# Two-block model on one core: the tensor engine's share of a depthwise convolution, as three products of exact parts instead of one in float32

## The chip, the cores and the metric

The kernel runs on one NeuronCore of one Trainium2 chip. The core has five engines, each with its own queue of instructions: TensorE (PE, with its weight loads as PEld), VectorE (DVE), ScalarE (ACT), GpSimd (POOL) and SyncE (SP), which issues the transfers of weights. The metric is the time of one execution in microseconds (us); lower is better.

## The reference, cut to what matters

The program is a chain of two transformer blocks on 256 tokens of width 1024. The first block has two layers; the second of these has a convolution module beside a cross-attention, and then a mixture of experts. The change lies in the convolution module alone: a gated projection, a causal depthwise convolution of width 31 over 768 channels, a layer norm and a swish.

```
def conformer_conv(glu_in, dw, dw_b, ln_g, ln_b):
    a, gate = jnp.split(glu_in, 2, axis=-1)
    u = a * jax.nn.sigmoid(gate)
    u = lax.conv_general_dilated(
        u, dw[:, None, :].astype(u.dtype), window_strides=(1,),
        padding=[(CONV_WIDTH - 1, 0)], dimension_numbers=('NWC', 'WIO', 'NWC'),
        feature_group_count=CONV_DIM) + dw_b.astype(u.dtype)
    return jax.nn.silu(layer_norm(u, ln_g, ln_b))
```

## The kernel before, in words

Every large product is done as three products of parts: a float32 operand is split into a high part of type fp32r (ACT copies it, which rounds) and a low part (DVE subtracts the high part from the original), and PE adds high by high, low by high and high by low (`mm3`). The weights are split on the way: SP loads a tile `wraw`, ACT writes `whi` (L107), DVE writes `wlo` (L122); slots come free as PE uses them.

The convolution stage works in six chunks of 128 channels, c = 0 to 5, with the channels on the partitions and the 256 tokens along the free side. For a chunk, `conv_in(c)` makes the gate and the value on PE (48 fp32r products, L1197 to L1199), ACT takes the sigmoid into `sg` (L1204), and DVE multiplies into `uT` (L1205, called u(c) below). The 31 taps of the depthwise convolution are then shared out: `PT = (11, 12, 12, 12, 13, 20)` taps of a chunk go to PE, as a float32 product of a diagonal matrix `dh` with a shifted window of `uT` (L1160), and the rest to DVE, one instruction a tap (L1170 to L1176). The diagonals are made by ACT from the identity and a tap's column in `dwc` (L1151), through a generator `dg` that is advanced ("pumped") at fixed places; they are made a chunk ahead. DVE adds PE's part to its own (`tap_end`, L1208).

In the loop over c, PE runs `conv_in(c + 1)` and then `pe_taps(c)`. Between these lies the cross-attention. Its keys and queries are normalised on DVE (`kn`, L533, after a power on POOL, L367), transposed on PE (L554) and copied by ACT into `mkT` and `mqT` (L555). Its four heads are advanced inside `pe_taps(2)` and later: PE makes logits (L564), DVE takes row maxima `mx` (L576), ACT takes the exponential `p` (L579). In front of `conv_in(2)` PE also runs the projection of the queries (L417 to L419 into two banks that `kn` of the keys reads first). After the six chunks DVE and ACT form sums for the layer norm, and PE adds them up (L1302 on), with a part of the output projection `og` as filler; the mixture of experts follows.

The program is recorded in the order in which it is written, and each engine works its own list in that order: nothing reorders it.

Of the kernel before, what the change touches and what calls it, by code (L numbers as in the profile page):

```python
# [10 lines left out]
F32 = mybir.dt.float32  # L11
F32R = mybir.dt.float32r
# [3 lines left out]
AF = mybir.ActivationFunctionType  # L16
OP = mybir.AluOpType
# [6 lines left out]
T = 256  # L24
# [7 lines left out]
PT = (11, 12, 12, 12, 13, 20)  # L32
# [131 lines left out]
def two_blocks(tc, A, out):  # L164
# [14 lines left out]
    def bank(i, shape=(128, 512)):  # L179
        return psp.tile(list(shape), F32, name=f"b{i}", tag=f"b{i}", bufs=1)  # L180

    V, S, G, PE = nc.vector, nc.scalar, nc.gpsimd, nc.tensor
# [92 lines left out]
    def pool(es, name, bufs, side=None):  # L275
        return es.enter_context(tc.tile_pool(name=name, bufs=bufs, side=side, reuse_waits="tile"))
# [15 lines left out]
    ident = const.tile([128, 128], F32, name="ident")  # L292
# [49 lines left out]
    dwc = const.tile([128, 6, 31], F32, name="dwc")  # L342
# [12 lines left out]
    def pc(name, j=0, n=128):  # L355
        return P[0:n, R[name] + j:R[name] + j + 1]
# [40 lines left out]
    def split(src, hi_, lo_):  # L397
        S.activation(hi_, src, AF.Copy)  # L398
        V.tensor_tensor(lo_, src, hi_.bitcast(F32), op=OP.subtract)  # L399

    def turn(*a):
        run(turns(*a))
# [18 lines left out]
    def gemm_col(o, xt, n, tbs=(0, 1), outer=False):  # L421

        th, tl = xt
        nu = 8 // (4 if n == 256 else 2)
        na = 8 // nu

        def one(u, i, tb):
            wh, wl = u
            for kk in range(na):
                k = i * na + kk  # L430
                mm3(o[tb], th[:, k, tb * 128:tb * 128 + 128], tl[:, k, tb * 128:tb * 128 + 128],
                    wh[:, kk, :], wl[:, kk, :], k == 0, k == 7)

        if outer:
            us = W.take(nu)
            for tb in tbs:
                for i, u in enumerate(us):
                    one(u, i, tb)
                    if tb == tbs[-1]:
                        W.done(1)  # L440
                    yield
        else:
            for i in range(nu):
                u = W.take(1)[0]
                for tb in tbs:
                    one(u, i, tb)
                    if tb == tbs[-1]:
                        W.done(1)
                    yield
# [199 lines left out]
    def mq_heads(i, o, mqT, ap, Tb):  # L649

        r = heads_stats(o, 4)

        def apply():
            qn = [ap.tile([128, 4, 64], F32, name="kn") for tb in range(2)]
            for tb in range(2):
                heads_apply(o[tb], r[:, 4 * tb:4 * tb + 4], 4, qn[tb])

            def fin():
                for tb in range(2):
                    heads_turn(qn[tb], 64, 4, gsc[0:64, 1 + i:2 + i], mqT, tb, bank(Tb[tb]))  # L660
            return fin
        return apply
# [22 lines left out]
    ap = pool(ph, "att", 2)  # L685
# [27 lines left out]
    o = [bank(4), bank(5)]  # L713
# [34 lines left out]
    o = [bank(2), bank(3)]  # L748
# [33 lines left out]
    o = [bank(0), bank(1)]  # L782
# [4 lines left out]
    o = [bank(2), bank(3)]  # L787
# [335 lines left out]
    ap = pool(pa, "att2", 2)  # L1123
# [17 lines left out]
    uT = cp.tile([128, 6, 30 + T], F32, name="uT")  # L1141
    G.memset(uT[:, :, 0:30], 0.0)
    vT = cp.tile([128, 6, T], F32, name="vT")
    diag = {}
    tapb = [bank(3)] * 5

    def diagonals(c):
        diag[c] = []
        for w in range(PT[c]):
            d = ap.tile([128, 128], F32, name="dh", bufs=33)  # L1150
            S.activation(d, ident, AF.Copy, scale=dwc[:, c, w:w + 1])  # L1151
            diag[c].append(d)
            yield

    def pe_taps(c):
        b = tapb[c]
        for w, d in enumerate(diag.pop(c)):
            if w % 4 == 3:
                yield
            PE.matmul(b[:, c % 2 * T:c % 2 * T + T], d, uT[:, c, w:w + T], start=w == 0, stop=w == PT[c] - 1)  # L1160
        return b

    def dve_taps(c):

        v2 = ap.tile([128, T], F32, name="v2")
        for w in range(PT[c], 31):
            wc = dwc[:, c, w:w + 1]
            d = vT[:, c] if (w - PT[c]) % 2 == 0 else v2
            if w == PT[c]:
                V.tensor_scalar(d, uT[:, c, w:w + T], wc, pc("dwb", c), op0=OP.mult, op1=OP.add)  # L1170
            elif w == PT[c] + 1:
                V.tensor_scalar(d, uT[:, c, w:w + T], wc, None, op0=OP.mult)
            else:
                V.scalar_tensor_tensor(d, uT[:, c, w:w + T], wc, d, op0=OP.mult, op1=OP.add)
            yield
        V.tensor_tensor(vT[:, c], vT[:, c], v2, op=OP.add)  # L1176
# [10 lines left out]
    def conv_in(c, tick):  # L1187

        b = bank(1 + c % 2)
        us = W.take(2)  # L1190
        for half in range(2):
            cc = slice(half * 128, half * 128 + 128)
            ob = b[:, half * T:half * T + T]
            for i, (wh, wl) in enumerate(us):
                for kk in range(4):
                    k = i * 4 + kk
                    PE.matmul(ob, wh[:, kk, cc], th[:, k], start=k == 0, stop=False)  # L1197
                    PE.matmul(ob, wh[:, kk, cc], tl[:, k], start=False, stop=False)
                    PE.matmul(ob, wl[:, kk, cc], th[:, k], start=False, stop=k == 7)  # L1199
                if half:  # L1200
                    W.done(1)
                tick()
        sg = ap.tile([128, T], F32, name="sg")
        S.activation(sg, b[:, T:2 * T], AF.Sigmoid, bias=pc("bin", 6 + c))  # L1204
        V.scalar_tensor_tensor(uT[:, c, 30:30 + T], b[:, 0:T], pc("bin", c), sg, op0=OP.add, op1=OP.mult)  # L1205

    def tap_end(c, b):
        V.tensor_tensor(vT[:, c], vT[:, c], b[:, c % 2 * T:c % 2 * T + T], op=OP.add)  # L1208

    dg = Bg(diagonals(0))  # L1210
    conv_in(0, lambda: dg.pump(3))
    later = mem_kv(1, om, mkT, mv, ap, (7, 4))
    for c in range(6):

        dt = Bg(dve_taps(c))
        dg.finish()
        if c < 5:
            dg = Bg(diagonals(c + 1))

        def tick():  # L1220
            dg.pump(3)
            dt.pump(3)
            heads.pump(1)

        if c + 1 == MQ_AT:
            o = [bank(5), bank(6)]
            for _ in gemm_col([o[0][:, 0:256], o[1][:, 0:256]], u1, 256):
                dt.pump(2)
        if c < 5:
            conv_in(c + 1, tick)  # L1230
        if c + 1 == MQ_AT:
            later()
            later = mq_heads(1, [o[tb][:, 0:256] for tb in range(2)], mqT, ap, (7, 0))
        else:
            if c < MQ_AT:
                later = later()
        if c == MQ_AT:
            later()
            mean = bank(0)
            heads = Bg(pipeline(jobs, 2))  # L1240
        if c == 5:
            tapb.append(bank(1))
        if c == 5:
            dt.pump(4)
        for i, _ in enumerate(pe_taps(c)):
            if c == 5 and i in (1, 2):
                turn(on[i - 1], 2, mix[0], mix[1], 6, i - 1, [4 + i])
            if c == 5 and i == 2:

                PE.matmul(mean[:, 0:T], ones, vT[:, 4], start=False, stop=True)  # L1250
            heads.pump(1)
            dt.pump(3)
        if c + 1 == MQ_AT:
            later = later()
        if MQ_AT <= c < 5:
            for x in ([c - 1] if c > MQ_AT else range(c)):
                PE.matmul(mean[:, 0:T], ones, vT[:, x], start=x == 0, stop=False)
        if c == 4:
            heads.finish()
            on = []  # L1260
            for tb in range(2):
                on.append(o_norm(ap, O, rinv, 0, 4, tb))
                dt.pump(3)
        dt.finish()
        if c < 5:
            tap_end(c, tapb[c])
# [32 lines left out]
    b = bank(2)  # L1299
# [8 lines left out]
    v = work.tile([128, 16], F32, name="var", bufs=4)  # L1308
# [5 lines left out]
    dg = work.tile([128, 512], F32, name="sq")[:, 0:T]  # L1314
# [8 lines left out]
    b = bank(3)  # L1323
# [121 lines left out]
    if NY:  # L1445
# [13 lines left out]
    b = bank(5)  # L1459
# [5 lines left out]
                           op0=OP.add, op1=OP.mult)  # L1465
# [190 lines left out]
    for e, fi in steps:  # L1656
# [53 lines left out]
        if prev is None:  # L1710
            def later(a=(sg, n, ht, [6, 7])):
                turn_pairs(*a)
# [79 lines left out]
    ap = pool(ph, "sec2", 2)  # L1792
# [33 lines left out]
    o = [bank(4), bank(5)]  # L1826
# [9 lines left out]
    for i in range(2):  # L1836
        V.scalar_tensor_tensor(lamr[:, 2 * i], lamr[:, 2 * i], 1.0, lamr[:, 2 * i + 1],
                               op0=OP.mult, op1=OP.mult, accum_out=nlam[:, i:i + 1])
# [14 lines left out]
    o = [bank(2), bank(3)]  # L1853
    run_with(gemm_col(o, u2, 512), {3: lambda: lq[0]([6, 7]), 5: lambda: lq[1]([6, 7])})
    lk = [plain(o[tb], tb, skT, 1.0) for tb in range(2)]
    o = [bank(0), bank(1)]
# [54 lines left out]
    for g in range(2):  # L1911
# [37 lines left out]
        for i in range(4):  # L1949
            hh = 4 * g + i  # L1950
            c = slice(hh * 64, hh * 64 + 64)
# [226 lines left out]
```

## Time and profile before

| | |
|---|---|
| median of 3 runs | 1802.96 us (1802.8 to 1804.41) |
| the profiled execution | 1803.33 us, of which the span of the trace is 1801.5 us |
| PE busy | 1766.6 us (98% of the span) |
| DVE busy | 1461.4 us (81%) |
| ACT busy | 1227.7 us (68%) |
| POOL busy | 68.4 us (4%) |
| HBM read | 504.93 MB, 281 GB/s over the span |

Busy time is the time in which at least one instruction of an engine is running. The ends of matmuls are modelled, so the pace of PE is read from the distance between starts. A time in the rows is counted from the start of the span. The convolution stage lies at about 370 to 470 us of the span.

### The profile page before, as it was taken

The numbers are of one execution on the slowest core, as the hardware profiler recorded it, in microseconds if no ns is written. First come the engines' busy times: TensorE is split into PE (matmuls) and PEld (weight loads), VectorE is DVE, ScalarE is ACT, GpSimd is POOL, SyncE is SP. The second block draws the span as 40 slices with busy tenths as digits, with TensorE's granted clock in tenths as the row PEclk, the third lists the DMA queues.
The fourth block names the chain that finished last, engine by engine and source line by source line (L and its number), as shares of the span: only waits on it lengthen the run. The fifth ranks groups of instructions, "written<-read, shape, count | busy, mean of one in ns | idle before, by whom it ended". The sixth has DMA issues, their size and how long they took to land. (4 is left out here: it accounts for less than half of the span.)

```text
span 1801.5 us, 23486 instructions
## 1 busy us (share of the span) xinstructions
PE 1766.6 (98%) x8620; PEld 1473.5 (82%) x8620; DVE 1461.4 (81%) x1759; ACT 1227.7 (68%) x1599; POOL 68.4 (4%) x100
## 2 busy tenths in 40 slices
PE   8999999999999999999999999999999999999998
PEld 6788888889788888888888888888888878778886
DVE  6556988688699999999999999999999974477553
ACT  5645544475488878877878788778787876656442
POOL 4200000000100000000000000000000010010000
PEclk9999999999999999999999999999999999999999
DMA  8325998562599999999999999999999744237540
GB/s 294 131 83 178 398 357 305 195 209 87 193 356 387 396 358 366 388 358 379 370 370 384 365 363 383 363 370 367 370 366 367 294 146 162 76 129 266 185 157 24
DMA packets 162891, 508.64 MB, mean 282 GB/s; under 512 B 8666, under 2 KB 26162, under 8 KB 148432
## 3 DMA queue, kind: packets, MB, share of 16 engines
q1 hardware_dynamic: 159376, 497.64, 74.6%
q0 software_dynamic: 3104, 8.91, 1.5%
q8 instruction: 69, 1.13, 0.2%
q10 hardware_dynamic: 288, 0.52, 0.1%
q14 instruction: 54, 0.44, 0.1%
HBM read 504.93 MB, written 2.11 MB: 281 GB/s over the span
## 5 line engine op out<-in xcount | busy, mean ns | idle before, releaser
L122 DVE TENSOR_TENSOR wlo<-wraw,whi 128x1024 fp32r<-128x1024 f32 (+1 forms) x894 | 1055.4, 1218 | 148.9 <-ACT whi L107 116.6
L107 ACT ACTIVATE whi<-wraw 128x1024 fp32r<-128x1024 f32 (+1 forms) x894 | 932.1, 1059 | 273.4 <-PE b L418 248.2
L417 PE MATMUL b<-whi,xeh 128*128 128x512 f32 x904 | 354.7, 392 | 0.0
L419 PE MATMUL b<-wlo,xeh 128*128 128x512 f32 x904 | 352.3, 390 | 0.0
L418 PE MATMUL b<-whi,xel 128*128 128x512 f32 x904 | 352.3, 390 | 0.0
L417 PE MATMUL b<-whi,xth 128*128 128x512 f32 (+2 forms) x656 | 255.4, 389 | 6.1 <-ACT xth L398 2.1
L417 PE MATMUL b<-whi,hth 128*128 128x512 f32 x656 | 258.0, 393 | 0.4 <-ACT hth L398 0.3
L418 PE MATMUL b<-whi,htl 128*128 128x512 f32 x656 | 255.7, 390 | 0.2 <-DVE htl L399 0.2
L419 PE MATMUL b<-wlo,hth 128*128 128x512 f32 x656 | 255.6, 390 | 0.0
L419 PE MATMUL b<-wlo,xth 128*128 128x512 f32 (+2 forms) x656 | 249.3, 380 | 2.5 <-DVE wlo L122 2.5
L418 PE MATMUL b<-whi,xtl 128*128 128x512 f32 (+2 forms) x656 | 249.2, 380 | 0.9 <-DVE xtl L399 0.7
L419 PEld LDWEIGHTS b<-wlo,xeh 128*128 128x128 f32 x904 | 169.7, 188 | 35.4
L418 PEld LDWEIGHTS b<-whi,xel 128*128 128x128 f32 x904 | 169.9, 188 | 34.3
L417 PEld LDWEIGHTS b<-whi,xeh 128*128 128x128 f32 x904 | 169.9, 188 | 34.3
L417 PEld LDWEIGHTS b<-whi,xth 128*128 128x128 f32 x656 | 124.1, 189 | 30.8 <-ACT xth L398 3.2
L419 PEld LDWEIGHTS b<-wlo,xth 128*128 128x128 f32 x656 | 123.9, 189 | 27.0 <-DVE wlo L122 4.2
L417 PEld LDWEIGHTS b<-whi,hth 128*128 128x128 f32 x656 | 123.3, 188 | 25.7 <-ACT whi L107 0.5
L419 PEld LDWEIGHTS b<-wlo,hth 128*128 128x128 f32 x656 | 123.2, 188 | 25.7
L418 PEld LDWEIGHTS b<-whi,xtl 128*128 128x128 f32 x656 | 124.1, 189 | 24.3 <-DVE xtl L399 3.0
L418 PEld LDWEIGHTS b<-whi,htl 128*128 128x128 f32 x656 | 123.3, 188 | 25.0 <-DVE htl L399 0.5
L398 ACT ACTIVATE hth<-b 128x512 fp32r<-128x512 f32 (+1 forms) x83 | 45.0, 591 | 61.9 <-PE b L410 61.9
L399 DVE TENSOR_TENSOR htl<-b,hth 128x512 fp32r<-128x512 f32 (+1 forms) x83 | 53.1, 678 | 31.7 <-ACT hth L398 31.1
(389 smaller groups left out, 1419.0 us busy)
## 6 DMA issues: line engine op xcount, KB each, us to landing
wraw<-in_moe_w_gate_dram SPq DMA_DIRECT2D x112, 1024.0 KB, 7.5
wraw<-in_moe_w_up_dram SPq DMA_DIRECT2D x112, 1024.0 KB, 7.5
wraw<-in_moe_w_down_dram SPq DMA_DIRECT2D x112, 1024.0 KB, 7.5
wraw<-in_w_ff_dram SPq DMA_DIRECT2D x32, 1024.0 KB, 5.2
adw<-in_ada_w_dram SPq DMA_DIRECT2D x24, 1024.0 KB, 7.7
wraw<-in_w_in_dram SPq DMA_DIRECT2D x12, 1024.0 KB, 5.0
wraw<-in_ffn_w_gate_dram SPq DMA_DIRECT2D x11, 1024.0 KB, 6.3
wraw<-in_ffn_w_up_dram SPq DMA_DIRECT2D x11, 1024.0 KB, 8.1
```

Of the source, the lines that this page charges most:

```text
L107: nc.scalar.activation(h, r, AF.Copy)
L122: self.nc.vector.tensor_tensor(l, r, h.bitcast(F32), op=OP.subtract)
L398: S.activation(hi_, src, AF.Copy)
L399: V.tensor_tensor(lo_, src, hi_.bitcast(F32), op=OP.subtract)
L417: PE.matmul(o, xh, wh, start=first, stop=False)
L418: PE.matmul(o, xl, wh, start=False, stop=False)
L419: PE.matmul(o, xh, wl, start=False, stop=last)
```

## The change

The tensor engine's taps are computed from parts, as the projections are. `uT` of a chunk is split into a tile `uhl` of two fp32r parts (ACT copies, DVE subtracts) right behind u(c); the tap columns are split once into `dws`; a diagonal has a high part (ACT) and a low part, which ACT makes for odd taps and GpSimd for even ones. A tap is then three fp32r products instead of one float32 product. The diagonals have 13 buffers of two parts instead of 33 of one, and a chunk's diagonals are pumped in the loop body of the same chunk (while `conv_in(c + 1)` is recorded) instead of one chunk ahead. The numbers of taps, DVE's taps and all else are as before.

```
+    dws = ap.tile([128, 2, 6, 31], F32R, name="dws", bufs=1)
+    split(dwc, dws[:, 0], dws[:, 1])
+    parts = {}
+
     def diagonals(c):
         diag[c] = []
         for w in range(PT[c]):
-            d = ap.tile([128, 128], F32, name="dh", bufs=33)
-            S.activation(d, ident, AF.Copy, scale=dwc[:, c, w:w + 1])
+            d = ap.tile([128, 2, 128], F32R, name="dh", bufs=13)
+            wh, wl = (dws[:, i, c, w:w + 1].bitcast(F32) for i in range(2))
+            S.activation(d[:, 0], ident, AF.Copy, scale=wh)
+            if w % 2:
+                S.activation(d[:, 1], ident, AF.Copy, scale=wl)
+            else:
+                G.tensor_scalar(d[:, 1], ident, wl, None, op0=OP.mult)
             diag[c].append(d)
             yield
 
     def pe_taps(c):
         b = tapb[c]
-        for w, d in enumerate(diag.pop(c)):
+        o = b[:, c % 2 * T:c % 2 * T + T]
+        x = parts.pop(c)
+        for w in range(PT[c]):
             if w % 4 == 3:
                 yield
-            PE.matmul(b[:, c % 2 * T:c % 2 * T + T], d, uT[:, c, w:w + T], start=w == 0, stop=w == PT[c] - 1)
+            while len(diag[c]) <= w:
+                dg.pump()
+            d = diag[c][w]
+            mm = ((d[:, 0], x[:, 0, w:w + T]), (d[:, 0], x[:, 1, w:w + T]), (d[:, 1], x[:, 0, w:w + T]))
+            for i, (a, v) in enumerate(mm):
+                PE.matmul(o, a, v, start=w + i == 0, stop=w == PT[c] - 1 and i == 2)
         return b
...
         V.scalar_tensor_tensor(uT[:, c, 30:30 + T], b[:, 0:T], pc("bin", c), sg, op0=OP.add, op1=OP.mult)
+        x = parts[c] = ap.tile([128, 2, 288], F32R, name="uhl")
+        G.memset(x[:, :, 0:30].bitcast(F32), 0.0)
+        split(uT[:, c, 30:30 + T], x[:, 0, 30:30 + T], x[:, 1, 30:30 + T])
...
         dt = Bg(dve_taps(c))
-        dg.finish()
-        if c < 5:
-            dg = Bg(diagonals(c + 1))
+        if c > 0:
+            dg = Bg(diagonals(c))
+            dg.pump(1 if c < 5 else 13)
```

On ACT, at the end of `conv_in(2)` (its sigmoid is `sg`), the list before has the copies into `mkT` and the squares `sq` of the queries right behind `sg`:

```order
L1151 ACTIVATE dh<-ident,dwc 128x128 x3
L1204 ACTIVATE sg<-b_3617,P 128x256 [waits PE_49,Activation_49]
L555 ACTIVATE mkT<-b_3715,P 64x4x128 [waits PE_49]
L555 ACTIVATE mkT<-b_3721,P 64x4x128 [waits PE_49]
L527 ACTIVATE sq<-b_3548 128x256 [waits Activation_49]
```

and now:

```order
L1159 ACTIVATE dh<-ident,dws 128x128
L1221 ACTIVATE sg<-b_3640,P 128x256 [waits PE_49,Activation_49]
L398 ACTIVATE uhl<-uT 128x256 [waits DVE_49,Pool_49]
L555 ACTIVATE mkT<-b_3751,P 64x4x128 [waits PE_49]
L555 ACTIVATE mkT<-b_3757,P 64x4x128 [waits PE_49]
L527 ACTIVATE sq<-b_3571 128x256 [waits Activation_49]
```

Between `sg` and `mkT` there now stands the copy of the high part, with a wait on DVE. A chunk later the same copy stands in front of `mqT`, the queries for the first head. Before:

```order
L1204 ACTIVATE sg<-b_3755,P 128x256 [waits PE_49,Activation_49]
L555 ACTIVATE mqT<-b_3854,gsc 64x4x128 [waits PE_49]
L555 ACTIVATE mqT<-b_3860,gsc 64x4x128 [waits PE_49]
L579 ACT_TABLE_LOAD
L579 ACTIVATE p,rinv<-b_3870,mx 128x256 [waits DVE_49]
```

Now:

```order
L1221 ACTIVATE sg<-b_3818,P 128x256 [waits PE_49]
L398 ACTIVATE uhl<-uT 128x256 [waits DVE_49]
L555 ACTIVATE mqT<-b_3930,gsc 64x4x128 [waits PE_49]
L555 ACTIVATE mqT<-b_3936,gsc 64x4x128 [waits PE_49]
L579 ACT_TABLE_LOAD
```

On DVE, at u(2), the list now has the subtraction for the low part (L399) between u(2) (L1222, formerly L1205) and the sums of squares `ssh` that lead to `kn`:

```order
L1193 TENSOR_TENSOR vT<-vT,v_3585 128x256 [waits DVE_49]
L1222 SCALAR_TENSOR_TENSOR uT<-b_3640,P,sg 128x256 [waits Activation_49]
L399 TENSOR_TENSOR uhl<-uT,uhl 128x256 [waits Activation_49]
L528 TENSOR_REDUCE ssh<-sq 128x4 [waits Activation_49] x2
L365 TENSOR_SCALAR var<-ssh 128x8 [waits DVE_49]
L533 TENSOR_TENSOR kn<-b_3571,rst 128x256 [waits PE_49,Pool_49]
```

It waits for ACT's copy, which itself waits for u(2); everything below it on DVE stands behind this. On PE, the first head's logits (L564) stand behind three taps of chunk 2, as before:

```order
L1177 MATMUL b_3317<-uhl,dh 128x256 [waits Activation_49] x2
L1177 MATMUL b_3317<-uhl,dh 128x256
L1177 MATMUL b_3317<-uhl,dh 128x256 [waits Pool_49]
L564 MATMUL b_3952<-mkT,mqT 128x256 [waits Activation_49]
L568 MATMUL b_3952<-mkT,mqT 128x256 [waits Activation_49]
L1177 MATMUL b_3317<-uhl,dh 128x256 x5
```

PE's place for them has not moved; what they wait for has, from behind `sg` to behind the copy.

## Rows read from the trace of the kernel before

**Rows 1.** Busy time by stretch: window, length, each engine (count), PEclk, DMA share, GB/s.
```profile
core 0: us, PE busy (x) PEld busy (x) DVE busy (x) ACT busy (x) POOL busy (x), PEclk, DMA share, GB/s
380.00:460.00 80.00, 79.16 (x515) 73.67 (x514) 70.51 (x160) 47.44 (x117) 3.17 (x2) 1.00 0.32 110
600.00:1200.00 600.00, 600.00 (x2745) 498.50 (x2745) 563.23 (x539) 483.82 (x510) 4.68 (x5) 1.00 0.98 371
492.50:500.00 7.50, 5.19 (x29) 4.89 (x29) 5.96 (x19) 4.59 (x5) 0.95 (x2) 0.54 0.90 286
```

**Rows 2.** Timeline of PE in the convolution stage: start, length, line, tiles, shapes, count.
```profile
375.72 0.28 PE L1199 MATMUL b<-xth,wlo 128*128 128x256 f32 x1
375.84 0.28 PE L1197 MATMUL b<-xth,whi 128*128 128x256 f32 x1
...
387.71 0.36 PE L417 MATMUL b<-whi,xth 128*128 128x256 f32 x1 [0.84 <-DVE kn L533]
...
411.97 1.46 PE L1160 MATMUL b<-uT,dh 128*128 128x256 f32 x6
413.27 0.60 PE L564 MATMUL b<-mkT,mqT 66*128 66x256 f32 x2
...
462.24 0.50 PE L1302 MATMUL b<-ones,vT 128*128 128x1 f32 x4
```

**Rows 3.** Instructions of the taps' line L1160: duration ns min/median/max, first and last start.
```profile
L1160 PE MATMUL b<-uT,dh x160: 376/378/435, 382.0 to 459.2; 128*128 128x256 f32 x160
```

**Rows 4.** Timeline of DVE, the instructions around u(c), with idle time before them.
```profile
378.36 0.48 DVE L1205 SCALAR_TENSOR_TENSOR uT<-b,P,sg 128x256 f32<-128x256 f32 x1 [3.09 <-ACT sg L1204]
...
403.95 0.48 DVE L1205 SCALAR_TENSOR_TENSOR uT<-b,P,sg 128x256 f32<-128x256 f32 x1
...
407.05 0.76 DVE L533 TENSOR_TENSOR kn<-b,rst 128x256 f32<-128x256 f32 x2 [1.76 <-POOL rst L367]
...
414.87 0.47 DVE L1205 SCALAR_TENSOR_TENSOR uT<-b,P,sg 128x256 f32<-128x256 f32 x1
415.26 0.41 DVE L576 TENSOR_REDUCE mx<-b 128x1 f32<-128x256 f32 x1
...
444.61 0.48 DVE L1205 SCALAR_TENSOR_TENSOR uT<-b,P,sg 128x256 f32<-128x256 f32 x1 [0.45 <-ACT sg L1204]
...
449.72 0.42 DVE L1208 TENSOR_TENSOR vT<-vT,b 128x256 f32<-128x256 f32 x1 [0.63 <-PE b L1160]
...
453.81 0.42 DVE L399 TENSOR_TENSOR xtl<-b,xth 128x256 fp32r<-128x256 f32 x1 [1.10 <-ACT xth L398]
...
460.53 0.41 DVE L1208 TENSOR_TENSOR vT<-vT,b 128x256 f32<-128x256 f32 x1
```

**Rows 5.** Timeline of ACT in the stage.
```profile
370.06 1.86 ACT L1151 ACTIVATE dh<-ident,dwc 128x128 f32<-128x128 f32 x6
...
390.74 1.06 ACT L107 ACTIVATE whi<-wraw 128x1024 fp32r<-128x1024 f32 x1 [4.65 <-PE b L418]
391.71 1.85 ACT L1151 ACTIVATE dh<-ident,dwc 128x128 f32<-128x128 f32 x6
...
400.19 1.24 ACT L555 ACTIVATE mkT<-b,P 64x512 f32<-64x512 f32 x2
401.33 0.63 ACT L527 ACTIVATE sq<-b 128x256 f32<-128x256 f32 x2
...
411.99 1.24 ACT L555 ACTIVATE mqT<-b,gsc 64x512 f32<-64x512 f32 x2
...
468.48 0.42 ACT L398 ACTIVATE xth<-vT 128x256 fp32r<-128x256 f32 x1
```

**Rows 6.** Timeline of POOL in the first 70 us.
```profile
38.95 0.20 POOL L760 COPY qa<-cs 128x8 f32<-128x8 f32 x1
...
51.22 2.92 POOL L367 TENSOR_TENSOR rst<-var,mhalf 128x16 f32<-128x16 f32 x1 [11.77 <-DVE var L365]
...
66.48 3.85 POOL L367 TENSOR_TENSOR rst<-var,mhalf 128x16 f32<-128x16 f32 x1 [10.46 <-DVE var L365]
```

**Rows 7.** Timeline of DVE at 66 us.
```profile
66.35 1.22 DVE L122 TENSOR_TENSOR wlo<-wraw,whi 128x1024 fp32r<-128x1024 f32 x1
```

## The prediction

> **What bounds the kernel now.** I read the busy time by stretch first. In the convolution stage (380 to 460 us) PE is busy 79.2 of 80 us at a granted clock of 1.00, DVE 70.5 and ACT 47.4; in the mixture of experts PE is busy all 600 of 600 us, so the transfers, with a share of 0.98 there, do not hold it [rows 1]. So a microsecond taken from PE's list in this stage moves everything behind it, as long as PE then finds its inputs ready, and DVE has only 9.5 us in 80 to be late in. Then I read PE's timeline for its pace, by starts, since ends are modelled: six float32 passes from 411.97 to 413.27, 0.216 us each, and an fp32r product of the same shape every 0.12 us [rows 2]. Then the instructions on DVE and ACT around u(c), for who waits for whom there [rows 4, 5]. The reader should see that DVE runs close behind PE: u(0) waits for the sigmoid 3.09 us, `tap_end` of chunk 4 waits for PE 0.63, and DVE's last addition ends at 460.94, only 1.3 us before PE starts the sums at 462.24 [rows 2, 4].
>
> **The change, part by part.** *PE.* The 80 taps are 160 passes now [rows 3], 160 x 0.216 = 34.6 us. They become 240 products of the form that runs at 0.12 (same shapes, the same pattern of a weight loaded twice and another once), 28.8 us. PE's own list gets 5.8 us shorter.
>
> *ACT.* New are 39 low diagonals, six copies of 128x256 and one of `dws`. A diagonal costs 0.30 (six in 1.86), a copy 0.42 [rows 5]: 39 x 0.30 + 7 x 0.42 = 14.6 us on an engine that has 32 us idle in 80 [rows 1]. The amount is hidden; what isn't hidden is the order. An engine's list is worked in order: ACT stood 4.65 us before a `whi` that waited for PE, and the diagonals behind it, which need nothing from PE, began only at 391.71 [rows 5].
>
> *DVE.* Six subtractions, each behind a copy on ACT that needs u(c) complete. Before, the row behind u(3) starts 0.39 us after it although u(3) lasts 0.47 [rows 4]: rows overlap by 0.08. Now u must end, ACT copies 0.42 [rows 5] with about 0.04 for each handover (an estimate), and the subtraction occupies about 0.35 (0.42 less the overlap). Each u(c) costs DVE 0.08 + 0.42 + 0.08 + 0.35 = 0.9 us, and DVE has nothing else to do in between.
>
> I follow the delay of DVE's list against before, since it grows faster than PE's saving:
> - In front of `sg`(0) ACT does the `dws` copy and five odd low diagonals, 6 x 0.30 = 1.8; DVE waits there for `sg` today [rows 4, 5], so all of it arrives: +1.8.
> - u(0) and u(1): +0.9 each, +3.6. Behind u(1) stands `kn` of the keys, for which PE's query projection waits 0.84 us even today, until 387.71 [rows 2]. PE would be there at 386.87 less 11 taps x 0.072 = 386.1, and starts at 391.3: 5.2 us idle.
> - u(2): +0.9; and the `mkT` pair (1.24) and the `sq` pair (0.63) [rows 5], done long before DVE came to them, now stand behind ACT's copy. From the copy's end they take some 1.8; DVE fills 0.7 of that with the subtraction and the first `ssh`, and waits 1.1. Delay at `kn` of the queries (407.05, still with its 1.76 us wait for POOL): +5.6.
> - u(3), 414.87 before, comes at 420.5. Behind it `mx` used to start 0.39 later. Now the chain is u 0.48, handover and copy 0.46, `mqT` pair 1.2, PE's logits 0.86 (two of 0.43, as from 413.27 [rows 2]) and a handover, 3.1 us: +2.7, +8.3 in all. PE, 3.6 late at the projection and 0.9 faster in `pe_taps(1)`, has finished its three taps at 415.7 and stands until 422.7: 6.9 us idle.
> - u(4), u(5): +0.9 each, +10.1.
> - With PE now ahead, DVE's waits for PE's results vanish: 0.45 + 0.63 + 1.10 [rows 4] = 2.2. +7.9.
> - The sums had 1.3 us of room behind DVE: 7.9 - 1.3 = +6.6 at 462.24, and what follows is the same chain.
>
> PE's 5.8 us are thus spent in waiting. The far end on the other side: if none of DVE's delays reached the sums, -5.8.
>
> *POOL.* 41 low diagonals and six small memsets. Nothing in the trace multiplies 128x128 there; the nearest plain operation, a copy of 128x8, takes 0.20, the farthest, a power of 128x16, 2.92 [rows 6]. I take 0.2 to 0.4 for a multiplication, which is the plain kind; six or seven in a chunk's 12 us or more are then hidden. At 2.92 they would need 18 to 20 us a chunk and hold PE by some 5 each, 1830; I keep that as the far end, hardly likely.
>
> *POOL beside DVE.* The power at 66.48 began while DVE subtracted two SBUF tiles (66.35, 1.22 us), and took 3.85 instead of 2.92, 0.93 more, about what DVE's instruction still had to run [rows 6, 7]. So the two do get in each other's way; whether DVE also waits for POOL no row shows. Some 35 of the 41 multiplications fall among DVE's taps, which read two SBUF tiles each. From nothing to a whole copy each, 35 x 0.2 = 7 us; I take 1, since only the other direction is seen. The Trainium skill speaks against this change here: its page "SBUF — State Buffer", section "SBUF: two separate sides", says that a DVE instruction with two SBUF inputs contends with a GpSimd instruction that reads SBUF, and that whichever starts second is blocked for the whole of the first. By that rule DVE would lose all 35 pieces. The trace agrees as far as POOL's 0.93 us of waiting go.
>
> *Clock.* In the stage the granted clock is 1.00; in the 7.5 us from 492.5, in which PE is busy 5.19, it is 0.54 [rows 1], so about 7 us of them at 1.2 GHz. Idle times of 5.2 and 6.9 us may bring such a fall. It costs between nothing, as PE is not last in most of the stage, and 3.5 us a fall; I take 1.
>
> Sum: +6.6 + 1 + 1 = +8.6 on the profiled execution's 1803.3 us (span 1801.5 and 1.8 around it). The median shown is 0.4 lower, so 1811.5.
>
> **The rivals.** *The saving goes through (faster).* DVE's 9.5 idle us take up its 6 x 0.9 = 5.4, and the copies into `mkT` and `mqT` do not come late because u(2) and u(3) do not. The time would be 1803 - 5.8 = 1797. For it: PE is the fullest engine, ACT and POOL have room. Against it: 1.76 of DVE's idle time is POOL's power and stays. It decides at u(3): if u(3) ends before PE has done its three taps of chunk 2, the heads wait for nothing.
>
> *No change.* The start and the copies cost what I count, but the two chains behind the copy (+1.1, +2.7) are hidden, because ACT finds u(2) and u(3) done: 6.6 - 3.8 = 2.8, without blocking or clock, 1806. Against it: DVE would have to reach u(3) some 2.7 us earlier than its list allows.
>
> *POOL blocks DVE fully.* Each multiplication among the taps costs DVE 0.2: +6.6 + 7 + 1, 1818. For it speaks the power that waited at 66.48 [rows 6, 7]; against it, that no row shows DVE waiting for POOL. It decides when most multiplications find DVE in the middle of its taps. (This is how the page "SBUF — State Buffer" of the Trainium skill would have it.)
>
> *The parts don't run at 0.12.* If a product with a window that starts at any column cost 0.216, PE would need 240 x 0.216 = 51.8, +17, 1820. Against it: shapes, types and loads are those of `conv_in`.
>
> **How the numbers follow.** 1807 to 1816 as summed: 0.50, with 1811.5 as its middle. POOL blocking, slow parts or slow multiplications, 1816 and more: 0.20. About as before, 1799.4 to 1806.6: 0.16. Faster, near 1797: 0.14. A measurement of this kernel can tell 0.2% (3.6 us) from no change. So faster 0.14, same 0.16, slower 0.70. The range leaves out the faster case and the far end: 1801 to 1821; the likeliest case's own is 1807 to 1816.
>
> **What would show it.** Right: fp32r taps 0.12 apart; ACT's copies `uhl` waiting for DVE's `uT`; PE idle some 5 us before the query projection, released by `kn`, and some 7 us before the first L564, released by ACT's `mqT`; the sums (L1302 before) near 469; a fall of the clock behind one of these. Wrong: PE without such waits and the sums near 456; or DVE's taps longer or further apart than now where POOL works, which would be the blocking; or PE waiting tap by tap for POOL's low parts.

## The result and the profile after

The median of the changed kernel is 1814.99 us (1811.64 to 1815.84, 4 runs), that of the kernel before, measured beside it, 1803.12 us (1802.80 to 1804.41, 4 runs): a ratio of 1.0059, with a 95% interval of 1.0048 to 1.0071. The change made the kernel slower. The profiled execution took 1811.64 us (span 1809.9), which is 8.3 us more than the profiled execution of before, where the sum had 8.6.

The profile of the changed kernel, busy time by stretch as in [rows 1]:

```profile
core 0: us, PE busy (x) PEld busy (x) DVE busy (x) ACT busy (x) POOL busy (x), PEclk, DMA share, GB/s
380.00:460.00 80.00, 70.06 (x531) 68.78 (x531) 65.81 (x145) 52.69 (x140) 31.37 (x39) 0.91 0.27 92
390.00:397.00 7.00, 6.43 (x33) 6.46 (x34) 6.86 (x17) 1.36 (x2) 0.00 (x0) 0.56 0.24 97
420.00:427.00 7.00, 5.03 (x20) 4.66 (x21) 4.24 (x12) 3.86 (x8) 1.66 (x2) 0.51 0.47 152
500.00:508.00 8.00, 5.46 (x31) 5.07 (x31) 6.60 (x21) 4.48 (x6) 1.77 (x3) 0.62 0.79 256
```

In the 80 us in which PE was busy 79.16 us before, it is busy 70.06 now, and DVE too has fallen, from 70.51 to 65.81. No engine became the bound: PE and DVE both wait more (the work in the window is not quite the same, as the stage has shifted). The granted clock, 1.00 throughout these 80 us before, is near its lower level (1.2 GHz) from 390 to 397 and from 420 to 427; the fall that stood at 492.5 before now stands at 500.

The timeline of PE in the changed kernel, with its idle time and what ended it:

```profile
368.68 0.39 PE L1214 MATMUL b<-xth,whi 128*128 128x256 f32 x1 [0.25 <-ACT xth L398]
...
380.89 4.10 PE L1177 MATMUL b<-uhl,dh 128*128 128x256 f32 x33
390.57 0.55 PE L417 MATMUL b<-whi,xth 128*128 128x256 f32 x1 [5.58 <-ACT whi L107]
...
416.30 1.31 PE L1177 MATMUL b<-uhl,dh 128*128 128x256 f32 x9
421.97 1.22 PE L564 MATMUL b<-mkT,mqT 66*128 66x256 f32 x2 [4.36 <-ACT mqT L555]
...
423.48 4.71 PE L1177 MATMUL b<-uhl,dh 128*128 128x256 f32 x24
428.03 0.60 PE L564 MATMUL b<-mkT,mqT 66*128 66x256 f32 x2
...
471.02 0.61 PE L1322 MATMUL b<-ones,vT 128*128 128x1 f32 x4 [1.15 <-DVE vT L1228]
```

The parts run as fast as hoped: 33 products in 4.10 us, 0.12 each. Then PE stands 5.58 us before the query projection and 4.36 before the first logits (L564). The low clock falls on what comes next: the 48 products of the projection take 8.27 us to the next `conv_in` instead of 5.83, and the 24 products from 423.48 to the next logits take 4.55 us instead of some 2.9 (24 x 0.12). The sums start at 471.02, 8.78 later than before [rows 2], although this stage's first product (368.68) came 1.06 us earlier than before's (369.74).

The timeline of DVE around u(c) (L1222):

```profile
379.12 0.48 DVE L1222 SCALAR_TENSOR_TENSOR uT<-b,P,sg 128x256 f32<-128x256 f32 x1 [3.37 <-ACT sg L1221]
...
388.38 0.47 DVE L1222 SCALAR_TENSOR_TENSOR uT<-b,P,sg 128x256 f32<-128x256 f32 x1
389.33 0.42 DVE L399 TENSOR_TENSOR uhl<-uT,uhl 128x256 fp32r<-128x256 f32 x1 [0.48 <-ACT uhl L398]
389.68 0.75 DVE L533 TENSOR_TENSOR kn<-b,rst 128x256 f32<-128x256 f32 x2
...
407.84 0.42 DVE L399 TENSOR_TENSOR uhl<-uT,uhl 128x256 fp32r<-128x256 f32 x1 [0.55 <-ACT uhl L398]
409.25 0.74 DVE L528 TENSOR_REDUCE ssh<-sq 128x4 f32<-128x256 f32 x2 [0.99 <-ACT sq L527]
...
412.00 0.76 DVE L533 TENSOR_TENSOR kn<-b,rst 128x256 f32<-128x256 f32 x2 [1.79 <-POOL rst L367]
...
420.42 0.47 DVE L1222 SCALAR_TENSOR_TENSOR uT<-b,P,sg 128x256 f32<-128x256 f32 x1
421.38 0.43 DVE L399 TENSOR_TENSOR uhl<-uT,uhl 128x256 fp32r<-128x256 f32 x1 [0.48 <-ACT uhl L398]
424.08 0.42 DVE L576 TENSOR_REDUCE mx<-b 128x1 f32<-128x256 f32 x1 [2.28 <-PE b L568]
...
429.10 0.42 DVE L576 TENSOR_REDUCE mx<-b 128x1 f32<-128x256 f32 x1 [1.74 <-PE b L568]
```

And that of ACT, the copies `uhl` and what stands behind them:

```profile
388.89 0.42 ACT L398 ACTIVATE uhl<-uT 128x256 fp32r<-128x256 f32 x1 [5.48 <-DVE uT L1222]
389.21 0.39 ACT L1157 ACTIVATE dh<-ident,dws 128x128 fp32r<-128x128 f32 x1
389.50 1.04 ACT L107 ACTIVATE whi<-wraw 128x1024 fp32r<-128x1024 f32 x1
...
420.93 0.42 ACT L398 ACTIVATE uhl<-uT 128x256 fp32r<-128x256 f32 x1 [3.92 <-DVE uT L1222]
421.25 1.24 ACT L555 ACTIVATE mqT<-b,gsc 64x512 f32<-64x512 f32 x2
```

ACT stands 5.48 and 3.92 us in front of a copy that waits for DVE, with work behind it. At the second place that work is `mqT`, and this is PE's wait of 4.36 us, seen from the engine that causes it. At the first place it is a `whi`, a weight that PE needs next, and the view names it as what PE waited for. But `kn` on DVE ended only 0.1 us before it (390.43 and 390.54), and the projection started 0.14 us after the end of `kn`, just as in the kernel before (387.57 and 387.71), where no `whi` was late:

```profile
386.83 0.74 DVE L533 TENSOR_TENSOR kn<-b,rst 128x256 f32<-128x256 f32 x2
```

So the late `whi` cost PE 0.1 us at most. The first wait is DVE's lateness at `kn`; the second is ACT's queue behind the copy.

### The profile page after: what moved, and what is told of

Its sections match the earlier page's. It is cut to its first block, busy times and chain, and to the rows that moved or that the text cites. A ratio compares the mean times of both kernels' runs of the same rounds, so it can differ in the third digit from the quotient of the medians.

```text
span 1809.9 us, 23801 instructions
## 1 busy us (share of the span) xinstructions
PE 1763.2 (97%) x8700; PEld 1473.4 (81%) x8700; DVE 1465.7 (81%) x1766; ACT 1241.6 (69%) x1645; POOL 104.9 (6%) x147
## 3 DMA queue, kind: packets, MB, share of 16 engines
q8 instruction: 70, 1.15, 0.2%
## 5 line engine op out<-in xcount | busy, mean ns | idle before, releaser
L399 DVE TENSOR_TENSOR htl<-b,hth 128x512 fp32r<-128x512 f32 (+1 forms) x83 | 53.2, 678 | 31.7 <-ACT hth L398 31.1
```

## The experiments

The times of a stage can be compared between executions only from a common point. In the table the columns are the start, in us of the span, of the stage's first product, of u(0) on DVE, of the query projection, of the first logits and of the sums on PE; then the time from first product to sums; then the ratio of the time to that of the kernel before, with its 95% interval. Each row is one profiled execution, the ratio is from all its runs.

| kernel | first | u(0) | projection | logits | sums | first to sums | ratio |
|---|---|---|---|---|---|---|---|
| before | 369.74 | 378.36 | 387.71 | 413.27 | 462.24 | 92.50 | 1 |
| after | 368.68 | 379.12 | 390.57 | 421.97 | 471.02 | 102.34 | 1.0059 (1.0048 to 1.0071) |
| split_only | 369.87 | 378.49 | 389.68 | 420.36 | 472.28 | 102.41 | 1.0052 (1.0036 to 1.0067) |
| no_split | 370.43 | 380.87 | 390.50 | 417.48 | 462.98 | 92.55 | 0.9998 (0.9989 to 1.0007) |
| late_split | 368.90 | 379.34 | 390.49 | 416.98 | 464.74 | 95.84 | 1.0028 (1.0018 to 1.0037) |
| late_fix | 370.45 | 380.89 | 390.70 | 416.46 | 462.87 | 92.42 | 1.0001 (0.9992 to 1.0010) |
| low_act | 370.29 | 382.78 | 393.96 | 424.78 | 476.11 | 105.82 | 1.0074 (1.0058 to 1.0089) |
| pool_twice | 370.36 | 380.80 | 392.25 | 423.73 | 474.93 | 104.57 | 1.0057 (1.0040 to 1.0073) |
| early | 372.78 | 383.30 | 394.76 | 426.17 | 474.96 | 102.18 | 1.0075 (1.0061 to 1.0089) |
| early_late | 376.19 | 385.89 | 395.71 | 421.24 | 467.87 | 91.68 | 1.0024 (1.0015 to 1.0033) |
| before_early | 370.21 | 378.24 | 387.61 | 413.15 | 462.12 | 91.91 | 0.9998 (0.9989 to 1.0007) |
| before_spread | 371.16 | 379.47 | 389.55 | 415.14 | 464.11 | 92.95 | 1.0005 (0.9996 to 1.0014) |
| spread | 369.05 | 377.61 | 387.43 | 413.00 | 459.66 | 90.61 | 0.9993 (0.9984 to 1.0001) |
| spread_pt | 369.19 | 377.76 | 387.57 | 412.41 | 459.17 | 89.98 | 0.9990 (0.9982 to 0.9999) |

The change adds 9.84 us between the first product and the sums. The theory says that this is DVE's waiting for ACT's copy, with what the copy holds up on ACT; the main rival, that the products, the diagonals or POOL beside DVE cost it.

**split_only: the split without the products.** The taps stay float32 as before, on POOL nothing is added.

```
 V.scalar_tensor_tensor(uT[:, c, 30:30 + T], b[:, 0:T], pc("bin", c), sg, op0=OP.add, op1=OP.mult)
+x = ap.tile([128, 2, 288], F32R, name="uhl", bufs=1)
+split(uT[:, c, 30:30 + T], x[:, 0, 30:30 + T], x[:, 1, 30:30 + T])
```

> The kernel before, with its float32 taps and diagonals, and the split of u(c) added at the place where the change has it; nothing reads the parts. Theory: the waits of DVE for the copy and those behind the copy on ACT come as with the change, and PE's 5.8 us did not matter there: sums at 468 to 471, 1808 to 1813. Rival A (POOL, diagonals or products cost it): within 2 us of before, 1801 to 1805.

Measured: 1813.76 us beside 1803.81. The waits in this kernel, summed from 366 to 480 us (who waits for whom, total, times, longest):

```profile
ACT uhl L398 <- DVE uT L1205: 13.0, 6, 5.0
...
PE b L564 <- ACT mqT L555: 5.0, 1, 5.0
...
DVE uhl L399 <- ACT uhl L398: 2.9, 6, 0.5
...
PE b L417 <- DVE kn L533: 2.7, 1, 2.7
```

ACT stands 13 us in front of its six copies, and PE has the two waits again, 2.7 us before the projection and 5.0 before the logits. It cost a little more than expected (sums at 472.28). Between first product and sums the split alone adds 9.91 us and the whole change 9.84, but that the two agree so well is chance, since they are made up differently. Here u(0) is not late (8.62 us after the first product, as before), there is no low clock behind the projection (its 48 products take 5.82 us), and PE, with its longer list, comes to the sums 1.3 us after DVE's last addition: 1.83 us of wait more at the projection, 4.97 at the logits, and 2.96 at the low clock behind them (7.28 us from the first head's logits to the second's, 4.32 before) make 9.8. In the changed kernel PE waits for DVE at the sums (1.15).

**no_split: the products without the split.** The opposite half: u(c) is rounded to fp32r by DVE as it is written, and the product with the low part reads zeros, so the low part of u is left out.

```
-split(uT[:, c, 30:30 + T], x[:, 0, 30:30 + T], x[:, 1, 30:30 + T])
+V.scalar_tensor_tensor(x[:, 30:30 + T], b[:, 0:T], pc("bin", c), sg, op0=OP.add, op1=OP.mult)
...
-(d[:, 0], x[:, 1, w:w + T])
+(d[:, 0], zero[:, w:w + T])
```

> The changed kernel without the split of u(c): DVE writes u(c) rounded to fp32r at once, the taps of both engines read that, and the product with the low part of u reads a tile of zeros, so that PE has the same 240 products. The low part of u is left out of the result. Theory: without the copy and the subtraction DVE is later than before by the start (0.8 us) and POOL (1.0 us) and earlier by up to 2.2 us of waits for PE; the sums start at 461 to 462 and the time is 1800 to 1803, some 2 us less than with the late split. Rival A (POOL beside DVE, diagonals or products cost it): 1808 or more. Rival B (PE's list is the bound once DVE is relieved): 1796 to 1798.

Measured: 1803.96 us, no difference from before, a microsecond above what was expected. All 240 products, all diagonals and POOL's multiplications are in it, so rival A falls. But PE's 5.8 us do not show either. PE waits 3.78 us before the projection (0.84 before), since u(0) still comes 1.82 us later after the first product than before (10.44 against 8.62) and PE is there sooner; and behind that wait the projection's 48 products take 8.33 us instead of 5.83, at a granted clock of 0.59 over 7 us. The two together, 2.94 and 2.50 us, are nearly all of the 5.8.

**late_split and late_fix: the split elsewhere.** Same work; only the place of the split in the lists changes.

```
-split(uT[:, c, 30:30 + T], x[:, 0, 30:30 + T], x[:, 1, 30:30 + T])
+pend.append(c)
...
 def tick():
+    if pend:
+        dt.pump(3)
+        late_split()
     dg.pump(3)
     dt.pump(3)
```

> The changed kernel, but the split of u(c) into its two parts is recorded later: on DVE behind three more taps of its own, on ACT behind the copies into mkT, sq and mqT. Work on every engine is the same. Theory (the cost is the waiting for ACT's copy, and what stands behind that copy on ACT): DVE's six waits of 0.5 us for uhl go (3.0 us), and PE's waits of 5.6 us for whi before the query projection and of 4.4 us for mqT before the first logits shrink below 2 us each; no fall of the clock is left between 380 and 430 us. DVE keeps six subtractions of 0.35 (2.1), the later start (0.8) and 1.0 us of POOL beside it, less the 2.2 us that it waited for PE before: the sums start near 463 and the time is 1802 to 1805. Rival A (the cost is POOL beside DVE, or the products themselves): 1810 to 1815 as with the change. Rival B (with the waits gone PE's 5.8 us go through): 1797 to 1799.

Measured: 1807.79 us, above the expected 1802 to 1805. The wait for `mqT` is gone, but PE still waits 4.37 us for `kn`. The edit itself had moved three more of DVE's taps ahead of each u(c + 1): from u(0) to u(1) it took 9.97 us, 9.26 with the change. In late_fix those three taps take the place of the tick's own (`else: dt.pump(3)`), and chunk 5's split stands behind the first three taps in `pe_taps(4)`.

> The late split again, without moving taps: the split takes its place behind the three taps that DVE does anyway at the first tick of the next projection (the run before had moved three more taps of each chunk ahead of u of the next one), and the split of chunk 5 stands behind three taps of chunk 4 and not behind 20 diagonals on ACT. Theory: the 1.2 us of those three taps at u(1) and PE's wait of 1.6 us for the parts of chunk 5 go; the later start (1.8 us at u(0)) stays, and with it a wait of PE of 3 to 4 us before the query projection: 1804 to 1807. Rival (the rest of the loss is POOL beside DVE and the products): 1807 to 1809.

Measured: 1803.73 us beside 1803.44, just under the expected range. The timeline of PE in late_fix:

```profile
390.70 0.58 PE L417 MATMUL b<-whi,xth 128*128 128x256 f32 x1 [3.02 <-DVE kn L533]
...
416.46 0.60 PE L564 MATMUL b<-mkT,mqT 66*128 66x256 f32 x2
416.89 0.61 PE L568 MATMUL b<-mkT,mqT 66*128 66x256 f32 x2
417.15 3.21 PE L1177 MATMUL b<-uhl,dh 128*128 128x256 f32 x24
420.20 0.60 PE L564 MATMUL b<-mkT,mqT 66*128 66x256 f32 x2
```

No wait stands in front of the logits now, and with no fall of the clock there the 24 products take 3.05 us. Putting the split elsewhere took back the whole of the loss. Beside no_split, which has neither copies nor subtractions (92.55 us from first product to sums, 92.42 here), the six copies and six subtractions as such cost nothing that can be measured. Both sides of the split were moved at once, on ACT and on DVE; what each gave by itself was not run.

**low_act: all low diagonals on ACT.** POOL's multiplication becomes `S.activation(d[:, 1], ident, AF.Copy, scale=wl)`.

> The changed kernel with all 80 low diagonals on ACT and none on POOL. Theory: the 1.0 us by which DVE's taps are lengthened beside POOL goes, ACT gets 41 x 0.30 = 12.3 us more, of which some 1.8 in front of the first sigmoid: 1810 to 1815, as with the change. Rival A (POOL holds DVE up): 1806 or less, with DVE's taps at 0.39 us apart throughout.

Measured: 1817.78 us, above the expected range. DVE's taps are 0.39 to 0.40 us apart throughout, so what POOL took from them is back; but ACT has six more diagonals ahead of the first sigmoid, u(0) comes 12.49 us after the first product (10.44 with the change), and that is more than was gained. Against the change the loss is not clear of noise (the two intervals overlap).

**pool_twice: POOL's multiplications doubled.**

```
 G.tensor_scalar(d[:, 1], ident, wl, None, op0=OP.mult)
+G.tensor_scalar(twice, ident, wl, None, op0=OP.mult)
```

> The changed kernel with every low diagonal on POOL made a second time, into a tile that nothing reads: 41 more multiplications of 0.75 to 1.0 us on POOL. Theory (POOL only lengthens a DVE tap now and then: 16 of 94 taps by 0.11 us in the changed kernel, about 1.2 us of pace in all): taps that are lengthened rise to about twice, 1 to 2 us more, and PE may wait up to 1 us for a low part: 1815 to 1819. Rival (a DVE instruction is held for the whole of POOL's multiplication): more than 10 us more, 1825 or above.

Measured: 1813.79 us, a little under the expected range and within the scatter of the change itself. From first product to sums it is 2.2 us more than with the change; PE waits for a low part three times in it, 1.4 us together. The longest of DVE's taps took 0.66 us and the mean rose from 0.488 to 0.496, so the rival falls.

**early, early_late, before_early: the start, first try.** The theory of the start said that ACT had too much ahead of the first sigmoid. So chunk 0's diagonals (and `dws`) were recorded in the product before the stage, in the change (early), in late_fix (early_late) and in the kernel before (before_early).

```
+    dg = Bg(diagonals(0))
+    for i, _ in enumerate(gemm_col(om, m1_["t"], 512)):
+        if i == 2:
+            turn(xs[0], 8, u1[0], u1[1], 0, 0, [2, 3])
+        dg.pump(2)
+    dg.finish()
```

> The changed kernel with only the early diagonals of chunk 0 and the early split of the tap columns; the split of u(c) stands where the change has it. Theory: the start's 1.8 us and up to 2 us more go, the waits behind the copy on ACT (1.0 at ssh, 2.7 at the first logits) and the subtractions stay: 3 to 5 us less than the change, 1809 to 1812. Rival (the start is hidden behind PE): 1813 to 1816.

> As late_fix, and the split of the tap columns and the diagonals of chunk 0 are recorded in the product before the stage (the cross-attention's keys and values of the memory), where ACT is idle 40 per cent of the time, so that ACT has nothing but weights ahead of the first sigmoid. Theory (DVE's start sets the stage, since DVE runs close behind PE to its end): u(0) comes 1.8 us earlier than with the change and up to 2 us earlier than before, PE's wait before the query projection falls under 2 us, there is no fall of the clock behind it, and part of PE's 5.8 us goes through: 1797 to 1802. Rival (ACT's new work before the stage delays the weights that PE waits for there): 1804 or more.

> The kernel before with the same one thing: the diagonals of chunk 0 are recorded in the product before the stage. Theory: DVE starts up to 2 us earlier, but PE is busy 79.2 of 80 us there, so only PE's 0.84 us before the query projection can go: 1801.5 to 1803.5. Rival (DVE is the bound in the stage even before): 1800 to 1801.

Measured: 1817.66, 1808.87 and 1803.23 us. early lies above its range and above its rival's; early_late missed, and its rival held; before_early came out as expected. The first product of early_late:

```profile
376.19 0.58 PE L1220 MATMUL b<-xth,whi 128*128 128x256 f32 x1 [4.31 <-ACT xth L398]
```

ACT was idle there only on average: the diagonals came between the norm and the copies `xth` on which the stage's first product waits. And u(0) still came 9.70 us after it (early_late), since a weight conversion ahead of the sigmoid waited 4.49 us. From first product to sums early_late was as quick as late_fix: 91.68 us (92.42).

**spread, spread_pt, before_spread: the start, second try.** Four of chunk 0's diagonals are recorded ahead of the first sigmoid instead of all eleven: `conv_in(0, lambda: dg.pump(1))` in place of `dg.pump(3)`, in late_fix (spread) and in the kernel before (before_spread). spread_pt also moves five taps from DVE to PE: `PT = (13, 13, 13, 13, 13, 20)`.

> The late split of the run before, and of chunk 0's diagonals only four are recorded ahead of the first sigmoid on ACT, the other seven behind it. Theory: the 1.8 us by which u(0) comes later than before go, and some more (11 ACTIVATEs fewer ahead of the sigmoid than in the change); PE's wait before the query projection falls from 3.0 us to under 1.5, no fall of the clock is left behind it; DVE is then ahead by about 2 us and the sums come 2 us earlier: 1800.5 to 1802.5. Rival (a weight conversion that waits on ACT ahead of the sigmoid sets the start): u(0) no earlier than before, 1802.5 to 1804.

> As spread, and five more taps go from DVE to PE: (13, 13, 13, 13, 13, 20) instead of (11, 12, 12, 12, 13, 20). Theory: a tap costs PE 0.36 us now and DVE 0.40; with DVE late and PE waiting, five taps take 2.0 us from DVE and give PE 1.8 of the time that it stood idle: 1 to 2 us less than spread, 1799 to 1801.5. Rival (PE is the bound once the waits are gone): as spread or up to 1.8 us more.

> The kernel before with the same one thing at its start: four of chunk 0's diagonals ahead of the first sigmoid, seven behind it. Theory: PE has only 0.84 us of idle time to give back there, since it is busy 79.2 of 80 us: 1802 to 1803.5. Rival (DVE bounds the stage before, too): 1800 to 1801.5.

Measured: 1802.40, 1801.34 and 1804.36 us, the last a microsecond above what was expected. PE in spread_pt:

```profile
385.65 1.91 PE L1177 MATMUL b<-uhl,dh 128*128 128x256 f32 x13 [0.66 <-POOL dh L1161]
...
387.57 0.38 PE L417 MATMUL b<-whi,xth 128*128 128x256 f32 x1
```

The projection waits for nothing any more and runs at the full clock; PE waits 0.66 us for POOL's low part and 0.29 us for DVE at the sums. From first product to sums it takes 89.98 us, 2.52 less than before. With 85 taps its list saves 34.6 - 255 x 0.12 = 4.0 us, so more than half of that goes through. In the time that is a ratio of 0.9990 with an interval that ends at 0.9999: faster by about a thousandth, at the edge of what can be told, and not told apart from spread. The same edit of the start does nothing for the kernel before; whether the five moved taps would do something for it was not run.

## Why the prediction was right, step by step

The forecast of slower, by DVE's and ACT's waits, held, and so did the place of each. The steps against the common point (to each delay the 1.06 us are added by which this stage began earlier):

- *PE's own list, 34.6 to 28.8 us:* right in pace, 33 products in 4.10 us. The rival of slow parts is out.
- *The start, +1.8 at u(0):* 10.44 - 8.62 = 1.82.
- *+3.6 at `kn` of the keys, PE idle 5.2:* the projection came 3.92 later and PE was idle 5.58. The view names a `whi` as the releaser, which stood behind ACT's copy of u(1) and which the prediction did not follow; it came 0.1 us after `kn`, so the path that was forecast is the one that set the time.
- *+5.6 at `kn` of the queries:* 412.00 - 407.05 + 1.06 = 6.0, with DVE's wait for `sq` 0.99 (1.1 forecast).
- *+2.7 behind u(3):* mis-sized. From u(3) to `mx` it took 424.08 - 420.42 = 3.66 instead of 0.39, so +3.27: the logits ran at the low clock, 1.22 us for a pair that took 0.60 before. PE's idle time there was 4.36 instead of 6.9, because PE had lost 2.4 us at the low clock from the projection on (8.27 us to the next `conv_in`, 5.83 before).
- *The clock, +1:* too small. Behind the two waits lie two falls, and the second kept DVE waiting for the logits of the second head too (1.74 us). With the 0.6 in the step above that is some 2 us; no kernel here has waits as long as these without a fall, so the two are not fully told apart.
- *u(4), u(5), the waits that vanish and the room, +10.1, -2.2, -1.3:* held. DVE's last addition came 470.55 - 460.53 + 1.06 = 11.1 later, where the steps with POOL's and the clock's 1 us had 9.9; the surplus is mostly the clock's, above. The three waits for PE are gone, and the sums came 9.84 later, so 1.2 of the 1.3 us of room was used.
- *POOL, 0.2 to 0.4 a multiplication:* wrong by more than twice; 41 of them took 0.89 on average. It was hidden, as the step said, because POOL had the time.
- *POOL beside DVE, +1:* about right. DVE's 94 taps of this form (L1191) average 0.475 us before and 0.488 after, 1.2 us in all. The rows of the taps' line in the changed kernel (durations in ns: least, median, most):

```profile
L1191 DVE SCALAR_TENSOR_TENSOR vT<-uT,dwc,vT x49: 471/478/588, 381.9 to 466.1; 128x256 f32<-128x256 f32 x49
L1191 DVE SCALAR_TENSOR_TENSOR v<-uT,dwc,v x45: 472/479/592, 382.3 to 465.4; 128x256 f32<-128x256 f32 x45
```

  No tap is held for a whole multiplication, of which the shortest took 0.60 us; the longest tap took 0.11 us more than the median. The Trainium skill's page "SBUF — State Buffer", section "SBUF: two separate sides", would have the second of the two blocked for the whole of the first. For POOL the trace agrees in kind (up to 2.58 us instead of 0.6), for DVE's taps it does not.

Together: 9.84 us from first product to sums, where the steps gave 6.6 + 1 + 1 = 8.6. From PE's side it is the same: PE waited 10.25 us more (5.58, 4.36 and 1.15 instead of 0.84), lost 2.44 us to the low clock behind the first wait and 2.32 behind the second (6.06 us from the first head's logits to the second's, 3.74 in late_fix), and saved 5.8, which makes 9.2 of the 9.84. That the profiled execution came out at +8.3, so near to the 8.6, is partly luck: the stage began 1.06 us earlier than before's.

What stays open is the rest of the median, which came 3.5 us above the forecast 1811.5: the other three executions of the changed kernel took 1814.9 to 1815.8 us, some 3.5 more than the profiled one. Their mean granted clock was 0.991, that of the profiled one 0.993; if the missing 0.002 of 1810 us is time at the lower level, it is worth some 3.6 us (an estimate, and a rough one, as both clocks are rounded). The profile of pool_twice, at 1814.3 us of span, has two stretches at a lower clock (0.72 from 115 to 121 us and from 1586 to 1592) where the changed kernel's has 1.00, both outside this stage; that the other three had these too was not seen. The first of the two lies ahead of all that the change touches.

## What to carry to other kernels

A cheaper product on the fullest engine can gain nothing, or lose, if its operand needs a copy that stands in two in-order lists: ask, for that copy, who waits for it, what is queued behind it on its engine, and whether it could be recorded later, when its input is long there and its reader still far off. Here that alone was worth the whole loss, with not an instruction less. Then look at the start of the stage: DVE ran close behind PE, and with 1.8 us of small work moved from ahead of the first sigmoid the stage took 90.61 us instead of 92.42 (spread and late_fix, one profile each). And an engine that is idle 40 per cent of the time can still be the wrong place for new work, when its next instruction is the one that others wait for.

## What the runs showed of the hardware

- A wait of PE can cost twice. In the changed kernel, with idle times of 5.58 and 4.36 us just before, the granted clock was 0.56 from 390 to 397 us and 0.51 from 420 to 427, and 24 products took 4.55 us instead of 3.05. In late_fix a wait of 3.02 us was followed by a fall too (0.76 from 390 to 397); in spread_pt, without the wait, there was none (1.00).
- Not each wait was followed by a fall. The same 48 products of the query projection took 5.82 us behind a wait of 2.67 (split_only) and 5.86 behind one of 1.54 (early_late), against 5.83 before; 7.14 behind 3.02 (late_fix), 8.33 behind 3.78 (no_split) and 8.27 behind 5.58 (the change).
- GpSimd multiplies 128x128 by a column in 0.60 us at best, and needs more beside DVE's long subtractions of two SBUF tiles: the longest of the 41, from 373.55, took 2.58 us, with DVE subtracting 128x1024 tiles from 373.38 to 375.74. DVE's taps lost at most 0.11 us each beside it (0.18 in pool_twice, with twice the multiplications).
